# Two-layer decoder trunk on one core: a rearranged opening with seven warm-up passes, and a seventh seven-product pair in the last down projection

## The chip, the cores and the metric

The kernel runs on one core of a Trainium2 chip. The metric is the device time of one execution, in microseconds (us). The times of the kernel before are three executions; one further execution was profiled, and every row shown below comes from it.

A core has five engines that run side by side, each its own list of instructions in order: TensorE (PE in the rows; its weight loads stand as PEld), VectorE (DVE), ScalarE (ACT), GpSimd (POOL) and SyncE (SP), which here only issues DMAs. Engines wait for each other through semaphores.

## The reference

The input is 256 tokens of 1024 features in float32. Each of two layers does, with weights of its own:

```
proj  = x @ w_in                      # q,k,v of 8 heads | q,k,v of 8 heads | two gates
A     = stick_breaking_attention(...) ;  B = softmax attention with partial rotary (...)
mix   = (sigmoid(g_sb) * (A @ w_branch_sb) + sigmoid(g_mb) * (B @ w_branch_moba)) @ w_out
x     = layer_norm(alpha * x + mix)
ffn   = (silu(x @ w_gate) * (x @ w_up)) @ w_down      # inner width 2816 = 22 chunks of 128
x     = layer_norm(alpha * x + ffn)
```

## The kernel before, in words

**Numbers.** Every product is made from two parts of each operand: `hi`, the operand rounded to fp32r, and `lo`, the rest. `mm3` makes one product as three passes through TensorE: hi by hi, hi by lo, lo by hi. Weights reach the chip as granules of 128 x 1024 values (512 KB), 122 to a layer. SyncE loads a granule into one of 6 `raw` buffers, ScalarE casts it to `whi` (a ring of 10 granules, L60 in the rows) and VectorE subtracts to give `wlo` (L65). Five granules of a layer take another way: GpSimd loads them straight into `whi` by DMA, ScalarE writes `wlo = -whi`, and a second DMA adds the raw weights to it (`BY_DMA`).

**Order.** The kernel is written with a manual schedule. A small planner, `Weave`, keeps an estimated clock for each engine, and from it decides where in each engine's list the side work (splits of weights, attention, norms) stands. The chip only sees the finished lists.

**The opening.** Ten matmuls on zeros (`N_WARM`, tile `busy`) occupy TensorE while the first loads are under way. ScalarE issues four loads of x (tiles `xT_raw`, called x00, x10, x01, x11: the token block, then the part of the features), and then loads its activation table and runs a one-element activation on it (`warm`). SyncE issues the first weights in halves (w00, w01, w10, ...) and the two larger remaining parts of x (x02, x12). `START` fixes in which order ScalarE and VectorE split those pieces. The first two outputs are v of the two attention kinds (`l0pv` from granules 0 to 3, then `l0pu` from granules 4 to 7), each for two token blocks. Granule 0 is not split (`NWHOLE = 1`): `whole` multiplies raw float32 values in one matmul, which stands as two rows in the profile. After them come q and k (`l0pq`).

**The down projection of layer 2.** It has 22 chunks. A chunk taken by itself is four products (two token blocks by two halves of the columns), so 12 passes. Two chunks taken as a pair (`seven_products`) need seven products in place of eight, so 21 passes, at the price of sums of weights and of activations on VectorE (`sums_line`, and the granule kinds "t" and "u", whose weights are first added up in the raw buffers). The table `DOWN[1]` gives the order: six pairs, and the rest single. The last `HOLD` chunks come after everything else, first for token block 0, then for block 1, so that the norm of block 0 runs beside the products of block 1. `combine_line` adds the four shared sums of the pairs (`one`, `six`, `five`, `seven`) into the residual rows `x0` and `x1` while those held chunks are multiplied. `last_first` and `last_second` then do the norm of the two token blocks and store them.

In rows, `l1pd`, `l1pe` and `l1pt` are the sums in PSUM of the last down projection, `l1hs` the sums of activations, `l1sf` the activations, `l1pv` and `l1pr` scratch of `combine_line`, `l1b_...` the last norm, `ln` its gain and shift.

Of the kernel before, what the change touches and what calls it, by code (L numbers as in the profile page):

```python
# [15 lines left out]
P = 128  # L16
# [14 lines left out]
GCOLS = 1024  # L31
NG_LAYER = 122
DOWN = ((0, (4, 5), (6, 7), 1, (8, 9), 2, (10, 11), 3, (12, 13), 14, 15, 16, 17, 18, 19, 20, 21),
        (0, (4, 5), (6, 7), 1, (8, 9), 2, (10, 11), 3, (12, 13), 16, (14, 15), 17, 18, 19, 20, 21))
STEPS = [[e for d in down for e in
          ([("n", d)] if isinstance(d, int) else [("b", d[1]), ("a", d[0]), ("t", d[0]), ("u", d[0])])]
         for down in DOWN]
BASE = [sum(NG_LAYER - NFC + len(x) for x in STEPS[:l]) for l in range(DEPTH + 1)]
EARLY = [*range(4), *range(16, 20), 8, 14, 9, 15, *range(4, 8), 20, 24, 21, 25, *range(10, 14), 22, 23,
         *range(26, 40)]  # L40
NACT = 12
# [67 lines left out]
class WeightStream:  # L109
# [2 lines left out]

    def __init__(self, nc, pool, w, total, weave, rings):
        self.nc, self.pool, self.w, self.total, self.weave = nc, pool, w, total, weave
        self.loaded, self.split = 0, NWHOLE
        self.done = -1
        self.free = {-1: 0.0}
        self.current = 0
        self.rings = rings
        self._lay()  # L120
        self.dma_t = 1.7
        self.raws, self.left = [], {0: 9.0}
        self.raw, self.parts, self.there, self.ready, self.dma = {}, {}, {}, {}, {}
# [50 lines left out]
    def by_dma(self, g):  # L174

        l, r = where(g)
        return r < NG_LAYER - NFC and r in BY_DMA[l] or self.aside(g)

    def aside(self, g):

# [3 lines left out]

    def put_aside(self, l, places):

        for g, parts in zip(filter(self.aside, range(BASE[l], BASE[l + 1])), places):
            self.parts[g] = parts
            self.dma[g] = self.weave.add(self.dma_line(g), self.weave.t)

    def dma_line(self, g):

        nc, weave = self.nc, self.weave
        hi, lo = self.parts[g]
        nc.gpsimd.dma_start(hi, self.w[place(g)], max_dma_last_dim=4096)
        yield weave.t + DMA_HI
        if self.aside(g):
            e = weave.pool(weave.t, nc.gpsimd.tensor_scalar, lo, hi.bitcast(F32), -1.0, None, op0=OP.mult) + 2.7
        else:
            e = weave.act(weave.t, GCOLS, nc.scalar.mul, lo, hi.bitcast(F32), -1.0)  # L200
        yield e
        nc.gpsimd.dma_start(lo, self.w[place(g)], accum_op=OP.add, max_dma_last_dim=4096)
        self.ready[g] = weave.t + DMA_LO

# [56 lines left out]
    def piece(self, g, i, e):  # L261

        if i == 0:
            self.parts[g] = tuple(ring[:, self.place[g]:self.place[g] + GCOLS] for ring in self.rings)
        (hi, lo), t, sl = self.parts[g], self.raw[g], self._pieces(g)[i]
        n = sl.stop - sl.start
        e = self.weave.act(e, n, self.nc.scalar.copy, hi[:, sl], t[:, sl])
        self.ready[g] = self.weave.dve(e, n, self.nc.vector.tensor_sub, lo[:, sl], t[:, sl], hi[:, sl].bitcast(F32))
        if sl.stop == GCOLS:
            self.raw.pop(g)  # L270
            self.left[g] = self.ready[g]
            self.split += 1
            self.load(g + 1 + NRAW)

# [6 lines left out]
    def take(self, g):  # L281
# [3 lines left out]
        while g in self.dma and g not in self.ready:  # L285
# [6 lines left out]
RING = 10 * GCOLS + LINES  # L292
NRAW = 6
NWHOLE = 1
START = (("x00", 4.4), ("x10", 5.4), ("x01", 6.4), ("w10", 6.4), ("w11", 7.4), ("x11", 7.4), ("w20", 8.2), ("x02", 9.0),
         ("w21", 9.7), ("x12", 10.3), ("w30", 11.0), ("w31", 11.7))
BY_DMA = ((18, 24, 28, 33, 38), (18, 24, 28, 33, 38))
ASIDE = ((), ())
X_AFTER = {(2, 0): (0, 2), (2, 1): (1, 2)}
NSPLIT = 10  # L300
HOLD = (8, 5)
FINE = 4
N_WARM = 10
LEAD = 2
LOAD = 1.46
DMA_HI = 6.0
# [12 lines left out]
def place(g):  # L319

    l, r = where(g)
    if r >= NG_LAYER - NFC:
        r = NG_LAYER - NFC + STEPS[l][r - (NG_LAYER - NFC)][1]
    return l * NG_LAYER + (EARLY[r] if r < len(EARLY) else r)


# [35 lines left out]
def hybrid_trunk_kernel(ctx: ExitStack, tc: tile.TileContext, w, xT_in, x_in, ln_in,  # L362
# [85 lines left out]
    def banksB(name):  # L448
        return psB.tile([P, 2, 512], F32, tag="B", name=name)
# [47 lines left out]

    kcs = [slice(0, 2), slice(2, 4), slice(4, 8)]
    ws.side = weave.add(ws.line(), last=True)
    for t, k in ((0, 0), (1, 0), (0, 1), (1, 1)):  # L500
        load_xT(t, kcs[k], nc.scalar)
    nc.scalar.activation(warm, zero, AF.Sigmoid)

    def between(g, i):
        if (g, i) in X_AFTER:
# [4 lines left out]
    for (kind, a, b), e in START:  # L510
        if kind == "x":
            split_xT(int(a), kcs[int(b)], e)
        else:
            ws.piece(int(a), int(b), e)
    weave.t = 4.5

    def late_loads():
        nc.sync.dma_start(ident, ident_in)
# [48 lines left out]

    def tok_major(o, g, t, first, last, k0):

        if g < NWHOLE:  # L570
            return whole(o, g, t, first)
        hi, lo = ws.take(g)
        hi = hi.rearrange("p (k c) -> p k c", k=2)
        lo = lo.rearrange("p (k c) -> p k c", k=2)
        for k in range(2):
            ts = slice(t * P, (t + 1) * P)
            mm3(o, xT_hi[:, k0 + k, ts], xT_lo[:, k0 + k, ts], hi[:, k, :], lo[:, k, :],
                first and k == 0, last and k == 1)

    def both_tokens(name, g0, put):  # L580

        acc = [banksB(f"{name}{t}")[:, 0, :] if g0 == 4 else bankM(f"{name}{t}", [P, WIDTH]) for t in range(2)]
        order = ((0, 0), (1, 0), (0, 1), (1, 1), (0, 2), (1, 2), (0, 3)) if g0 <= 4 else \
            ((0, 0), (0, 1), (0, 2), (1, 0), (1, 1), (0, 3), (1, 2))
        for t, k in order + ((1, 3),):
            tok_major(acc[t], g0 + k, t, k == 0, k == 3, 2 * k)
            if t == 1:
                ws.used(g0 + k)
            if k == 3:
                put(t, acc[t])  # L590

    def feat_major(o, g):

# [332 lines left out]
    def load_gb(l, i):  # L926
        tiles = []
        for j in range(2):
            tiles.append(unit(f"ln{l}{i}{j}", [P, D]))

        def late():
            for j, a in enumerate(tiles):
                nc.sync.dma_start(a, ln_in[4 * l + 2 * i + j].partition_broadcast(P))
                ws.dma_t = max(ws.dma_t, weave.t) + LOAD

        return tiles, late
# [3 lines left out]
    for l in range(DEPTH):  # L940
# [10 lines left out]
            split_v(v_mb[t], ps)  # L951

        if l == 0:
            both_tokens(f"{L}pv", G, put_v)
            both_tokens(f"{L}pu", G + 4, put_u)
        else:
            for t in range(2):
                weave.finish(norms[:t + 1])
                pe_after(xT_ready[t])
                for j, put in enumerate((put_v, put_u)):  # L960
                    ps = bankM(f"{L}pvu{j}{t}", [P, WIDTH])
                    for i in range(4):
                        g = G + 4 * j + i
                        tok_major(ps, g, t, i == 0, i == 3, 2 * i)
                        if t == 1:
                            ws.used(g)
                    put(t, ps)
# [164 lines left out]

        pairs = [d for d in DOWN[l] if not isinstance(d, int)]
        pair_of = {c: i for i, p in enumerate(pairs) for c in p}
        raw_h, sums, h_there = {}, {}, {}

        def sums_line(i, e):

# [4 lines left out]
                                (3, b0, tmp[:, 1], OP.subtract)):  # L1143
                e = dve(e, P, nc.vector.tensor_tensor, tmp[:, j], x, y, op=op)
            if i < 2:
                both = wide_work(f"{L}hw{i}", F32R).rearrange("p a h c -> p (a h c)")[:, :GCOLS]
            elif i < 4:
                both = work.tile([P, 2, 2, S], F32R, tag=("sbq", "sbk")[i - 2],
                                 name=f"{L}hw{i}").rearrange("p a h c -> p (a h c)")
            if i < 4:  # L1150
                places = [[both[:, n * 512:(n + 1) * 512].rearrange("p (j c) -> p j c", c=P) for n in range(2)]]
            elif i == 4:
                places = [[x[:, 2:, :].rearrange("p k (j c) -> p (k j) c", c=P) for x in h_t[-1]]]
            elif i == 5:
                places = [[x[:, 0::2, P:] for x in h_t[k]] for k in (1, 2)]
            else:
                places = [[x[:, 6:, :].rearrange("p k (j c) -> p (k j) c", c=P) for x in (xT_hi, xT_lo)]]
            n = 4 // len(places)
            sums[i] = [[hi_lo[m][:, j] for hi_lo in places for j in range(n)] for m in range(2)]
            yield e  # L1160
# [75 lines left out]
        def seven_products(i, g, late_half):  # L1236
# [22 lines left out]
            into(c21, hb[:, t1], lb[:, t1], m_hi[:, one_], m_lo[:, one_])  # L1259
            ws.used(g + 3)  # L1260

        def combine_line(e):

            v, r = (small_work(f"{L}{n}", [P, 512]) for n in ("pv", "pr"))
# [1 line left out]
            e = act(e, 512, nc.scalar.copy, v, six)  # L1266
            yield e
            e = dve(e, 512, nc.vector.tensor_sub, v, one, v)
            m_free[bank_of(one)] = m_free[bank_of(six)] = residual(e, x0, halves[0], one)
            e = dve(e, 512, nc.vector.tensor_add, r, seven, v)  # L1270
            e = dve(e, 512, nc.vector.tensor_add, v, five, v)
# [7 lines left out]
        for n, d in enumerate(DOWN[l][:-HOLD[l]]):  # L1279
            if n == 5:  # L1280
                late()
            if isinstance(d, int):
                chunk(banks[0], g, d, 0)
                chunk(banks[1][:1], g, d, 1)

                def half(g=g, d=d):
                    chunk(banks[1][1:], g, d, 1)
                    ws.used(g)

                if n == 0:  # L1290
                    late_half.append(half)
                else:
                    half()
                g += 1
                continue
# [110 lines left out]
```

## Time and profile before

| | |
|---|---|
| three executions | 716.02, 716.48, 716.57 us (median 716.48) |
| the profiled execution: time, span | 716.68 us, 714.9 us |
| TensorE matmul busy, of the span | 706.7 us, 99% |
| VectorE, ScalarE, GpSimd busy | 599.5 us, 436.6 us, 35.0 us |
| moved by DMA | 141.58 MB, 198 GB/s on average |

The span reaches from the first to the last instruction; the time of an execution is about 1.8 us more. In the timeline a row has its start, its length, the engine, the source line, the operation with tiles and shapes, a count where equal rows follow each other, and in brackets how long the engine had been idle before it and what ended that. TensorE's rows overlap, since a matmul's end is modelled: its pace is read from the distance between starts.

### The profile page before, as it was taken

How to read it: one execution, taken by the hardware profiler on the slowest of the kernel's cores; microseconds unless marked ns; L12 is line 12 of the kernel's file. 1: busy time of each engine (PE TensorE's matmuls, PEld its weight loads, DVE VectorE, ACT ScalarE, POOL GpSimd, SP SyncE). 2: the span in 40 equal slices, each digit the busy share in tenths (PEclk: the TensorE clock that was granted, in tenths of full speed). 3: DMA queues.
4: the chain of work that ended last, by engine and by line, in shares of the span. 5: the costliest groups of instructions: out<-in, count | busy, mean ns of one | idle time of the engine just before them, and what ended most of it. 6: DMA issues, size and time to landing. Idle time of an engine off the chain costs nothing. (4 is left out here: it accounts for less than half of the span.)

```text
span 714.9 us, 13082 instructions
## 1 busy us (share of the span) xinstructions
PE 706.7 (99%) x5135; PEld 657.7 (92%) x5135; DVE 599.5 (84%) x920; ACT 436.6 (61%) x677; POOL 35.0 (5%) x61
## 2 busy tenths in 40 slices
PE   9999999999999999999999999999999999999995
PEld 7999999998899999988889999999888999999885
DVE  5989989797888777799887899987879878778987
ACT  5868977664565554456456787876456555544551
POOL 0200100000000000000000010000010000000002
PEclk9999999999999999999999999999999999999998
DMA  8977755565585664449559566745646856524451
GB/s 319 396 230 254 198 153 173 167 217 186 171 301 197 194 194 145 122 142 329 198 183 315 155 186 170 213 142 177 237 147 216 273 189 198 191 96 137 147 206 59
DMA packets 40526, 141.58 MB, mean 198 GB/s; under 512 B 4625, under 2 KB 5393, under 8 KB 40465
## 3 DMA queue, kind: packets, MB, share of 16 engines
q1 hardware_dynamic: 37008, 129.74, 53.1%
q0 software_dynamic: 2880, 10.49, 6.9%
q8 instruction: 40, 0.66, 0.4%
q10 hardware_dynamic: 576, 0.52, 0.2%
q14 instruction: 22, 0.17, 0.1%
HBM read 139.69 MB, written 1.05 MB: 197 GB/s over the span
## 5 line engine op out<-in xcount | busy, mean ns | idle before, releaser
L65 DVE TENSOR_TENSOR wlo<-raw,whi 128x1024 fp32r<-128x1024 f32 (+1 forms) x274 | 302.2, 1125 | 27.2 <-ACT whi L60 23.8
L60 ACT CAST whi<-raw 128x1024 fp32r<-128x1024 f32 (+1 forms) x274 | 260.2, 973 | 75.1 <-DVE raw L65 29.5
L529 PE MATMUL l0pf<-xT_hi,whi 128*128 128x256 f32 x288 | 79.6, 276 | 0.0
L529 PE MATMUL l1pf<-xT_hi,whi 128*128 128x256 f32 x288 | 79.6, 276 | 0.0
L529 PE MATMUL l0pf<-xT_lo,whi 128*128 128x256 f32 x288 | 79.5, 276 | 0.0
L529 PE MATMUL l0pf<-xT_hi,wlo 128*128 128x256 f32 x288 | 79.5, 276 | 0.0
L529 PE MATMUL l1pf<-xT_hi,wlo 128*128 128x256 f32 x288 | 79.5, 276 | 0.0
L529 PE MATMUL l1pf<-xT_lo,whi 128*128 128x256 f32 x288 | 79.5, 276 | 0.0
L529 PEld LDWEIGHTS l0pf<-xT_lo,whi 128*128 128x128 f32 x288 | 54.1, 188 | 0.0
L529 PEld LDWEIGHTS l1pf<-xT_lo,whi 128*128 128x128 f32 x288 | 54.1, 188 | 0.0
L529 PEld LDWEIGHTS l1pf<-xT_hi,whi 128*128 128x128 f32 x288 | 54.1, 188 | 0.0
L529 PEld LDWEIGHTS l0pf<-xT_hi,whi 128*128 128x128 f32 x288 | 54.1, 188 | 0.0
L529 PEld LDWEIGHTS l0pf<-xT_hi,wlo 128*128 128x128 f32 x288 | 54.1, 188 | 0.0
L529 PEld LDWEIGHTS l1pf<-xT_hi,wlo 128*128 128x128 f32 x288 | 54.1, 188 | 0.0
L529 PE MATMUL l0pg<-xT_hi,whi 128*128 128x256 f32 x128 | 35.8, 280 | 0.0
L529 PE MATMUL l1pg<-xT_hi,whi 128*128 128x256 f32 x128 | 35.8, 280 | 0.0
L529 PE MATMUL l0pg<-xT_hi,wlo 128*128 128x256 f32 x128 | 35.5, 277 | 0.0
L529 PE MATMUL l1pg<-xT_hi,wlo 128*128 128x256 f32 x128 | 35.5, 277 | 0.0
L529 PE MATMUL l1pg<-xT_lo,whi 128*128 128x256 f32 x128 | 35.5, 277 | 0.0
L529 PE MATMUL l0pg<-xT_lo,whi 128*128 128x256 f32 x128 | 35.5, 277 | 0.0
L65 DVE TENSOR_TENSOR l1sf<-l1sf,l1pf 128x256 f32<-128x256 f32 x36 | 15.1, 421 | 15.5 <-ACT l1sf L60 14.9
L60 ACT ACTIVATE l0sf<-l0pf 128x256 f32<-128x256 f32 x18 | 6.9, 385 | 31.2 <-PE l0pf L529 31.2
(485 smaller groups left out, 1941.0 us busy)
## 6 DMA issues: line engine op xcount, KB each, us to landing
raw<-in_w_dram SPq DMA_DIRECT2D x230, 512.0 KB, 4.2
whi<-in_w_dram POOLq DMA_DIRECT2D x10, 512.0 KB, 5.1
wlo<-in_w_dram POOLq DMA_DIRECT2D x10, 512.0 KB, 6.3
ln<-in_ln_dram SPq DMA_DIRECT2D x8, 512.0 KB, 5.9
raw<-in_w_dram SPq DMA_DIRECT2D x8, 256.0 KB, 4.6
x<-in_x_dram SPq DMA_DIRECT2D x2, 512.0 KB, 4.7
xT_raw<-in_xT_dram ACTq DMA_DIRECT2D x4, 128.0 KB, 4.8
xT_raw<-in_xT_dram SPq DMA_DIRECT2D x2, 256.0 KB, 5.1
```

The costliest lines, as they stand in the source:

```text
L60: f(*args, **kw)
L65: f(*args, **kw)
L529: nc.tensor.matmul(o, a, b, start=start, stop=stop)
```

## The change

1. Seven warm-up matmuls in place of ten. ScalarE loads its activation table and runs `warm` right after its first load of x, ahead of the other three.
2. Granule 0 is taken whole for token block 0 only; for block 1 it is split like the others. The two v outputs are made alternately, so the granules of the first layer now come in the order `FIRST` (0 of one, 0 of the other, 1, 1, ...), and their sums stand in two wide PSUM tiles (`banksB`). The larger parts of x are loaded two halves later, and `START` is rearranged.
3. Layer 2's down projection: a seventh pair (16, 17); the chunks 2 and 3 come by DMA into the space of `xT_hi` and `xT_lo` (`ASIDE`); four held chunks in place of five. Three of the final sums into x are done by GpSimd, after ScalarE has multiplied those rows by alpha (`alpha_line`).
4. In both layers the gain and shift of the second norm are loaded through GpSimd's queue in place of SyncE's.

```diff
-        (0, (4, 5), (6, 7), 1, (8, 9), 2, (10, 11), 3, (12, 13), 16, (14, 15), 17, 18, 19, 20, 21))
+        (0, (4, 5), (6, 7), 1, (8, 9), 2, (10, 11), (12, 13), 3, (14, 15), (16, 17), 18, 19, 20, 21))
+FIRST = [0, 16, 1, 17, 2, 18, 3, 19]
...
-            self.dma[g] = self.weave.add(self.dma_line(g), self.weave.t)
+            self.dma[g] = self.weave.add(self.dma_line(g), self.weave.t + 3.0 * i)
...
-        if self.aside(g):
-            e = weave.pool(weave.t, nc.gpsimd.tensor_scalar, lo, hi.bitcast(F32), -1.0, None, op0=OP.mult) + 2.7
-        else:
-            e = weave.act(weave.t, GCOLS, nc.scalar.mul, lo, hi.bitcast(F32), -1.0)
+        yield weave.act(weave.t, GCOLS, nc.scalar.mul, lo, hi.bitcast(F32), -1.0)
...
-START = (("x00", 4.4), ("x10", 5.4), ("x01", 6.4), ("w10", 6.4), ("w11", 7.4), ("x11", 7.4), ("w20", 8.2), ("x02", 9.0),
-         ("w21", 9.7), ("x12", 10.3), ("w30", 11.0), ("w31", 11.7))
+START = (("x00", 4.2), ("w00", 4.7), ("x10", 5.5), ("w01", 5.6), ("w10", 6.2), ("w11", 7.0), ("w20", 7.7), ("x01", 7.8),
+         ("w21", 8.3), ("x11", 8.5), ("w30", 9.4), ("w31", 10.4), ("x02", 10.6), ("x12", 11.2))
-ASIDE = ((), ())
-X_AFTER = {(2, 0): (0, 2), (2, 1): (1, 2)}
+ASIDE = ((), (2, 3))
+X_AFTER = {(3, 0): (0, 2), (3, 1): (1, 2)}
-HOLD = (8, 5)
+HOLD = (8, 4)
-N_WARM = 10
+N_WARM = 7
...
-    for t, k in ((0, 0), (1, 0), (0, 1), (1, 1)):
+    load_xT(0, kcs[0], nc.scalar)
+    nc.scalar.activation(warm, zero, AF.Sigmoid)
+    for t, k in ((1, 0), (0, 1), (1, 1)):
         load_xT(t, kcs[k], nc.scalar)
-    nc.scalar.activation(warm, zero, AF.Sigmoid)
...
-        if g < NWHOLE:
+        if g < NWHOLE and t == 0:
             return whole(o, g, t, first)
...
+        both = [banksB(f"{names[0]}{t}") for t in range(2)]
+        acc = [[two[:, n, :] for two in both] for n in range(2)]
+        for i in range(4):
+            for n in range(2):
+                for t in range(2):
+                    tok_major(acc[n][t], g0 + 2 * i + n, t, i == 0, i == 3, 2 * i)
+                    if i == 3:
+                        puts[n](t, acc[n][t])
+                ws.used(g0 + 2 * i + n)
...
-                nc.sync.dma_start(a, ln_in[4 * l + 2 * i + j].partition_broadcast(P))
+                (nc.gpsimd if i else nc.sync).dma_start(a, ln_in[4 * l + 2 * i + j].partition_broadcast(P))
...
+        def pool_add(e, x, y, op):
+            pool(e, nc.gpsimd.tensor_tensor, x, x, y, op=op)
+            weave.pool_t += 1.0
+
+        def alpha_line():
+            for x, c in ((xs[0], halves[1]), (xs[1], halves[0]), (xs[1], halves[1])):
+                act(weave.t, 512, nc.scalar.mul, x[:, c], x[:, c], ALPHA)
+                yield weave.t + 4.0
...
+            if l == DEPTH - 1:
+                w = small_work(f"{L}pw", [P, 512])
+                e2 = dve(e, 512, nc.vector.tensor_add, w, five, v)
+                pool_add(e2, x0[:, halves[1]], w, OP.subtract)
+                m_free[bank_of(one)] = m_free[bank_of(six)] = residual(e, x0, halves[0], one)
+                e = dve(e, 512, nc.vector.tensor_add, r, seven, v)
+                pool_add(e, x1[:, halves[0]], r, OP.add)
+                e = dve(e, 512, nc.vector.tensor_sub, v, five, r)
+                pool_add(e, x1[:, halves[1]], v, OP.subtract)
+                return
```

What stands in the engines' lists at three places follows. TensorE's list begins with the warm-up matmuls and goes on with the first output. Before:

```order
L487 MATMUL busy<-few 128x128 x10
L564 MATMUL l0pv_173<-raw_119,xT_raw_92 128x512 x2
L564 MATMUL l0pv_174<-raw_119,xT_raw_93 128x512 x2
L529 MATMUL l0pv_173<-whi,xT_hi 128x512
L529 MATMUL l0pv_173<-wlo,xT_hi 128x512
L529 MATMUL l0pv_173<-whi,xT_lo 128x512
```

After (`l0pv_174` is now the tile of token block 0, `l0pv_175` that of block 1):

```order
L489 MATMUL busy<-few 128x128 x7
L567 MATMUL l0pv_174<-raw_116,xT_raw_92 128x512 x2
L532 MATMUL l0pv_175<-whi,xT_hi 128x512
L532 MATMUL l0pv_175<-wlo,xT_hi 128x512
L532 MATMUL l0pv_175<-whi,xT_lo 128x512
```

Three warm-up matmuls and two raw matmuls are gone, and the split parts of granule 0 and of x10 are needed right after the first two raw matmuls.

ScalarE's list at the pair (8, 9) of layer 2's down projection, with the numbers of the granules (242 and 243 are the pair's two raw buffers, each cast twice). Before:

```order
L60 CAST whi_89<-raw242_7171 128x1024
L60 CAST whi_89<-raw243_7294 128x512
L60 CAST whi_89<-raw243_7294 128x1024
L60 CAST whi_89<-raw242_7171 128x1024
L60 CAST whi_89<-raw246_7296 128x1024
```

After:

```order
L61 CAST whi_89<-raw242_7174 128x1024
L61 CAST whi_89<-raw243_7304 128x512
L61 ACTIVATE xT_lo_86<-xT_hi_85 128x1024
L61 CAST whi_89<-raw243_7304 128x1024
L61 ACTIVATE xT_lo_86<-xT_hi_85 128x1024
L61 CAST whi_89<-raw242_7174 128x1024
```

The two activations for chunks 2 and 3 stand between the casts of this pair, and the cast of a single chunk (246) is gone.

VectorE's list after its last split of weights, with `x_87` and `x_88` the rows of the two token blocks. Before:

```order
L65 TENSOR_TENSOR l1pv<-l1pd_7404,l1pv 128x512
L65 SCALAR_TENSOR_TENSOR x_87<-x_87,l1pd_7404 128x512
L65 TENSOR_TENSOR l1pr<-l1pt_7408,l1pv 128x512
L65 TENSOR_TENSOR l1pv<-l1pt_7407,l1pv 128x512
L65 SCALAR_TENSOR_TENSOR x_87<-x_87,l1pv 128x512
L65 SCALAR_TENSOR_TENSOR x_88<-x_88,l1pr 128x512
L65 TENSOR_TENSOR l1pr<-l1pt_7407,l1pr 128x512
L65 SCALAR_TENSOR_TENSOR x_88<-x_88,l1pr 128x512
L65 SCALAR_TENSOR_TENSOR x_87,l1b_st_7735<-x_87,l1pd_7403 128x512 x2
```

After:

```order
L66 TENSOR_TENSOR l1pv<-l1pd_7414,l1pv 128x512
L66 TENSOR_TENSOR l1pw<-l1pt_7417,l1pv 128x512
L66 SCALAR_TENSOR_TENSOR x_87<-x_87,l1pd_7414 128x512
L66 TENSOR_TENSOR l1pr<-l1pt_7418,l1pv 128x512
L66 TENSOR_TENSOR l1pv<-l1pt_7417,l1pr 128x512
L66 SCALAR_TENSOR_TENSOR x_87,l1b_st_7758<-x_87,l1pd_7413 128x512 x2
```

Eight operations ahead of the norm have become five; the three sums into x that are missing stand on GpSimd now.

More of the change, by code (lines that the diff above doesn't have):

```diff
@@ L114, in __init__ @@
         self.nc, self.pool, self.w, self.total, self.weave = nc, pool, w, total, weave
-        self.loaded, self.split = 0, NWHOLE
+        self.loaded, self.split = 0, 0
         self.done = -1
@@ L176, in by_dma @@
         l, r = where(g)
-        return r < NG_LAYER - NFC and r in BY_DMA[l] or self.aside(g)
+        if r >= NG_LAYER - NFC:
+            return self.aside(g)
+        return r in BY_DMA[l]
     def aside(self, g):
@@ L185, in put_aside @@
     def put_aside(self, l, places):
-        for g, parts in zip(filter(self.aside, range(BASE[l], BASE[l + 1])), places):
+        for i, (g, parts) in enumerate(zip(filter(self.aside, range(BASE[l], BASE[l + 1])), places)):
             self.parts[g] = parts
-            self.dma[g] = self.weave.add(self.dma_line(g), self.weave.t)
+            self.dma[g] = self.weave.add(self.dma_line(g), self.weave.t + 3.0 * i)
     def dma_line(self, g):
@@ L196, in dma_line @@
         yield weave.t + DMA_HI
-        if self.aside(g):
-            e = weave.pool(weave.t, nc.gpsimd.tensor_scalar, lo, hi.bitcast(F32), -1.0, None, op0=OP.mult) + 2.7
-        else:
-            e = weave.act(weave.t, GCOLS, nc.scalar.mul, lo, hi.bitcast(F32), -1.0)
-        yield e
+        yield weave.act(weave.t, GCOLS, nc.scalar.mul, lo, hi.bitcast(F32), -1.0)
         nc.gpsimd.dma_start(lo, self.w[place(g)], accum_op=OP.add, max_dma_last_dim=4096)
@@ L269, in piece @@
         if sl.stop == GCOLS:
-            self.raw.pop(g)
-            self.left[g] = self.ready[g]
+            if g >= NWHOLE:
+                self.raw.pop(g)
+                self.left[g] = self.ready[g]
             self.split += 1
@@ L323, in place @@
         r = NG_LAYER - NFC + STEPS[l][r - (NG_LAYER - NFC)][1]
+    if l == 0 and r < len(FIRST):
+        return FIRST[r]
     return l * NG_LAYER + (EARLY[r] if r < len(EARLY) else r)
@@ L514, in hybrid_trunk_kernel @@
             ws.piece(int(a), int(b), e)
-    weave.t = 4.5
+    weave.t = 5.1
     def late_loads():
@@ L578, in tok_major, with both_tokens @@
                 first and k == 0, last and k == 1)
[L580 to L590, printed above, removed]
+    def both_tokens(names, g0, puts):
+        both = [banksB(f"{names[0]}{t}") for t in range(2)]
[7 more added lines that the diff above has]
+                ws.used(g0 + 2 * i + n)
     def feat_major(o, g):
@@ L953, in hybrid_trunk_kernel @@
         if l == 0:
-            both_tokens(f"{L}pv", G, put_v)
-            both_tokens(f"{L}pu", G + 4, put_u)
+            both_tokens((f"{L}pv", f"{L}pu"), G, (put_v, put_u))
         else:
@@ L1134, in hybrid_trunk_kernel @@
         pair_of = {c: i for i, p in enumerate(pairs) for c in p}
-        raw_h, sums, h_there = {}, {}, {}
+        raw_h, sums, h_there, wides = {}, {}, {}, []
         def sums_line(i, e):
@@ L1145, in sums_line @@
             if i < 2:
-                both = wide_work(f"{L}hw{i}", F32R).rearrange("p a h c -> p (a h c)")[:, :GCOLS]
+                both = wide_work(f"{L}hw{i}", F32R).rearrange("p a h c -> p (a h c)")
+                wides.append(both[:, GCOLS:])
             elif i < 4:
@@ L1156, in sums_line @@
             else:
-                places = [[x[:, 6:, :].rearrange("p k (j c) -> p (k j) c", c=P) for x in (xT_hi, xT_lo)]]
+                places = [[x.rearrange("p (j c) -> p j c", c=P) for x in wides]]
             n = 4 // len(places)
@@ L1268, in combine_line @@
             e = dve(e, 512, nc.vector.tensor_sub, v, one, v)
+            if l == DEPTH - 1:
[5 more added lines that the diff above has]
+                pool_add(e, x1[:, halves[0]], r, OP.add)
+                e = dve(e, 512, nc.vector.tensor_add, v, five, r)
+                pool_add(e, x1[:, halves[1]], v, OP.subtract)
+                return
             m_free[bank_of(one)] = m_free[bank_of(six)] = residual(e, x0, halves[0], one)
@@ L1281, in hybrid_trunk_kernel @@
                 late()
+                if l == DEPTH - 1:
+                    weave.start(alpha_line())
             if isinstance(d, int):
```

## The prediction

> **What bounds the kernel now.** I read the page first, for the busy shares, then what TensorE waited for, then the timeline of the two places that the change touches: the first 28 us and the last 60 us.
>
> ```profile
> span 714.9 us, 13082 instructions
> PE 706.7 (99%) x5135; PEld 657.7 (92%) x5135; DVE 599.5 (84%) x920; ACT 436.6 (61%) x677; POOL 35.0 (5%) x61
> ...
> PE busy L487 <- DVE few L484: 0.9, 1, 0.9
> ...
> 686.22:693.70 7.48, 7.48 (x34) 1.00 0.85 343
> ```
>
> TensorE is busy for 99%, and in the list of waits it has one entry, 0.9 us before its first instruction. So the time is the number of passes times their pace, plus what happens ahead of the first useful pass and behind the last one. The window row, inside the last pair, gives the pace: 33 passes start in it (the 34th reaches in from before) in 7.48 us, 0.227 us for a pass over 512 columns. A change pays only by passes that go, by an earlier start, or by a shorter tail; work on other engines costs nothing until it makes TensorE wait.
>
> The opening:
>
> ```profile
> 0.91 3.36 PE L487 MATMUL busy<-few 128*128 128x128 f32 x14 [0.91 <-DVE few L484]
> ...
> 0.91 3.97 PE L487 MATMUL busy<-few 128*128 128x128 f32 x17 [0.91 <-DVE few L484]
> ...
> 0.91 4.30 PE L487 MATMUL busy<-few 128*128 128x128 f32 x20 [0.91 <-DVE few L484]
> ...
> 4.26 0.40 ACT L60 CAST xT_hi<-xT_raw 128x256 fp32r<-128x256 f32 x1
> 5.05 0.59 PE L564 MATMUL l0pv<-raw,xT_raw 128*128 128x512 f32 x1
> 5.48 0.19 PEld L564 LDWEIGHTS l0pv<-raw,xT_raw 128*128 128x128 f32 x1 [0.24 <-DMA raw<-in_w_dram]
> 5.65 0.41 ACT L60 CAST xT_hi<-xT_raw 128x256 fp32r<-128x256 f32 x1 [0.99 <-DMA xT_raw<-in_xT_dram]
> 5.91 0.19 PEld L564 LDWEIGHTS l0pv<-raw,xT_raw 128*128 128x128 f32 x1 [0.24 <-issue]
> ...
> 12.61 0.19 PEld L529 LDWEIGHTS l0pv<-whi,xT_hi 128*128 128x128 f32 x1 [0.28 <-ACT xT_hi L60]
> 13.33 0.19 PEld L529 LDWEIGHTS l0pv<-whi,xT_lo 128*128 128x128 f32 x1 [0.43 <-DVE xT_lo L65]
> ...
> 27.97 0.28 PE L529 MATMUL l0pq<-xT_hi,whi 128*128 128x256 f32 x1
> ```
>
> The first three rows are three views, which end at 4.05, at 4.69 and open: 14 of the 20 warm-up rows have started by 4.05, 17 by 4.69, and the other three start between 4.69 and the first useful row at 5.05. So the pace is 0.21 us up to about 4.70 and 0.12 after it: TensorE runs at half speed for its first 3.8 us. x00 is there at 4.26, w01 by 5.48, x10 at 5.65. The raw rows follow at 0.43 us. v and u take 27.97 - 5.05 = 22.92 us: 8 x 0.43 = 3.44, 84 passes x 0.227 = 19.04, and 0.44 left over, which the rows at 12.61 and 13.33 explain (x12 is late).
>
> **The change part by part: the opening.** Three warm-up matmuls are six rows; without them TensorE is free at 4.06, and its first useful row waits for x00, at 4.26 in place of 5.05: -0.79. The rows from 4.26 to 4.70 run at half speed: +0.22. Two raw matmuls go (4 rows, 1.72) and six passes come (1.36): -0.36. The waits for x12 go (-0.44): its first use moves from the third granule to the fifth, past 15 us. The splits of v come some 6 us later, in banks that nobody waits for. That is -1.37 if nothing else waits, and v and u end at 26.60.
>
> What is late next is the splitting, since the alternating order needs w10 and w11 at once, and granule 0 now adds two casts and two subtractions. By the rows below a half granule costs 0.62 on ScalarE and 0.68 on VectorE behind it.
>
> ```profile
> 7.12 1.13 ACT L60 CAST whi<-raw 128x512 fp32r<-128x512 f32 x2
> 9.31 0.68 DVE L65 TENSOR_TENSOR wlo<-raw,whi 128x512 fp32r<-128x512 f32 x1
> 14.43 1.05 ACT L60 CAST whi<-raw 128x1024 fp32r<-128x1024 f32 x1 [0.63 <-DMA raw<-in_w_dram]
> 15.51 2.52 DVE L65 TENSOR_TENSOR wlo<-raw,whi 128x1024 fp32r<-128x1024 f32 x2 [0.98 <-ACT whi L60]
> 2.61 1.28 ACT L502 ACT_TABLE_LOAD   x1 [2.61 <-issue]
> ```
>
> The first raw matmul ends at 4.70 + 0.86 - 0.22 = 5.34 and the second needs w01: +0.14, to 6.34. Block 1 of granule 0: x10 is cast by 6.05, w01 by 6.67, its low part is there at 7.35, wanted at 7.25: +0.10. Granule 1: w11 is there by 7.64 (the second cast of the 7.12 row), its low part at 7.64 + 0.62 + 0.04 + 0.68 = 8.98, wanted near 8.74: +0.24. The fifth granule lands at 14.43, its low part is there at 15.51 + 1.26 = 16.77, wanted near 16.5: 0 to 0.3, I take 0.17. Together +0.65. The opening gives -1.37 + 0.65 = -0.72.
>
> The table load ahead of x10, x01 and x11 is the part that no row shows. If ScalarE goes on issuing behind a running table load, x10 leaves at 1.17 as now and nothing changes; if it waits for load and activation (1.28 + 0.20), x10 comes up to 1.5 us later, and so do its cast and the casts behind it: block 1 of granule 0 starts at 7.57 in place of 6.34, +1.23. Nor is a gain excluded: with x10, x01 and x11 out of the way, w01 to w11 land sooner and the waits shrink. I take no change, between -0.48 and +1.23.
>
> **Layer 2's down projection.** One product less is 3 passes: -0.68. Everything else must stay hidden, and VectorE is the engine to watch:
>
> ```profile
> L65 DVE TENSOR_TENSOR l1hs<-l1sf,l1hs x12: 283/288/293, 567.8 to 622.7; 128x128 f32<-128x128 f32 x12
> 635.87 0.42 DVE L65 TENSOR_TENSOR l1sf<-l1sf,l1pf 128x256 f32<-128x256 f32 x1 [1.81 <-ACT l1sf L60]
> 651.40 0.28 PE L529 MATMUL l1pf<-xT_hi,wlo 128*128 128x256 f32 x1
> 655.82 1.57 ACT L60 CAST whi<-raw 128x1024 fp32r<-128x1024 f32 x2 [1.92 <-PE l1pe L529]
> 656.91 1.83 DVE L65 TENSOR_TENSOR wlo<-raw,whi 128x1024 fp32r<-128x1024 f32 x2 [0.84 <-ACT whi L60]
> 660.28 1.06 ACT L60 CAST whi<-raw 128x1024 fp32r<-128x1024 f32 x1 [2.88 <-DVE raw L65]
> 661.56 5.38 DVE L65 TENSOR_TENSOR wlo<-raw,whi 128x1024 fp32r<-128x1024 f32 x5
> 669.76 5.38 DVE L65 TENSOR_TENSOR wlo<-raw,whi 128x1024 fp32r<-128x1024 f32 x5
> 671.26 0.39 PE L529 MATMUL l1pd<-whi,l1h_hi 128*128 128x512 f32 x1
> 686.16 2.50 DVE L65 TENSOR_TENSOR wlo<-raw,whi 128x1024 fp32r<-128x1024 f32 x2
> 692.34 0.39 PE L529 MATMUL l1pd<-whi,l1h_hi 128*128 128x512 f32 x1
> ...
> 696.80 0.68 DVE L65 TENSOR_TENSOR l1pv<-l1pd,l1pv 128x512 f32<-128x512 f32 x1
> 702.10 0.68 DVE L65 SCALAR_TENSOR_TENSOR x<-x,l1pd 128x512 f32<-128x512 f32 x1
> 706.73 2.50 POOL L70 TENSOR_TENSOR l1b_y<-l1b_y,ln 128x512 f32<-128x512 f32 x2 [0.83 <-ACT l1b_y L60]
> 707.65 0.42 DVE L65 TENSOR_TENSOR x<-x,l1b_rest 128x256 f32<-128x256 f32 x1
> DMA to landing us min/median/max: 3.7/5.1/8.3
> ```
>
> From 656.91, where the ring lets it go on (ScalarE's cast at 655.82 waits for TensorE), VectorE runs without a break; a pair with a single chunk takes 669.76 - 661.56 = 8.20 us, while TensorE needs 33 x 0.227 = 7.48. Its lead has shrunk to 692.34 - 688.66 = 3.7 us at the last pair's last product. A split is about 1.17, so a pair alone is 7.03 against 21 passes, 4.76. In before's clock (the opening's gain moves both engines): pair (8, 9) is split by 664.0; the activation for chunk 3 on ScalarE stands between its last two casts, whose gap was only 0.4, so +0.45. Four more pairs: 664.4 + 4 x 7.03 = 692.6, and +0.2 where an alpha multiplication (about 0.6, the length of a 512-wide cast) stands in front of a cast: 692.8. TensorE's last pair ends at 693.70 - 0.68 + 12 x 0.227 = 695.74, since 12 passes fewer are held back behind it, and wants that last part 6 passes earlier, at 694.4. The lead falls to 1.6 us and stays over zero: cost 0.
>
> The chunks 2 and 3: their space is free when `l1pf` ends, 651.40; the two first DMAs land after 5.1 us (the last row, of the same kind of DMA in the attention parts), near 657, when ScalarE comes to them at 657.4. The adding DMA follows; TensorE wants chunk 2 at 671. The sums of the seventh pair (four of 0.29, one 0.68) fall where VectorE sat idle before 635.9 for 1.81 us. The norm's gain and shift leave SyncE's queue, which costs nothing as GpSimd's queue is empty there.
>
> The end: block 0's held chunks are 24 passes in place of 30 and end at 695.74 + 5.44 = 701.18; they are `combine_line`'s cover. VectorE: 692.8 + 4 x 1.17 = 697.5, then five operations in 3.4: 700.9, where it came to the norm at 702.10 before, 1.2 behind TensorE (693.70 + 30 x 0.227 + 0.39). GpSimd's three sums, at 1.25 each (the 706.73 row) from 699.0, end at 702.8; block 1's rows are wanted 12 passes after 701.18, at 704. So the end is again TensorE's last pass: the sum at 707.65 moves by the full 0.68, and the tail behind it is as before. Bounds for this stage: -0.75 (a tail with less crowding on GpSimd) to +0.3 (below).
>
> **The sum.** 716.68 (the profiled execution) - 0.72 - 0.68 = 715.28. That execution is 0.20 above the median, so 715.1 for the median of the changed kernel, 1.4 below. About 0.2%, 1.43 us or 715.05, is what a measurement can tell from no change; the forecast lies at that line.
>
> **The rivals.**
>
> *The opening loses its waits.* If x10, x01 and x11 leave later without being missed, w01, w10 and w11 come sooner and most of the 0.65 goes: 715.1 - 0.5 = 714.6. For it: the loads share the DMA engines, and x01 and x11 are wanted only after 10 us now. Against it: the fifth granule's landing stays.
>
> *x10 comes late.* ScalarE's queue holds x10 until its table is loaded: +1.23 less the 0.3 that is already counted as waiting, 716.0. No row shows a DMA behind a table load on this queue.
>
> *VectorE falls behind.* The first DMA may land after 8.3 us, the longest above, at 660.1: both casts behind the activations slip, 1.5 us in all, against 0.5 of slack at the end: 715.1 + 1.0 = 716.1. Against it: that landing was seen beside a crowded DMA queue.
>
> *TensorE stays at half speed, the slower case.* The rows show full speed only after 3.8 us of unbroken passes. Now there is a gap from 4.06 to 4.26 and shorter ones at 5.34, 7.25 and 8.74. If a gap starts the count again, half speed until t costs (t - 4.70) / 2, less the 0.5 of waits that it hides. If only the first gap does, t is 8.05: +1.2, 716.3. If the one at 8.74 does too, t is about 12.5: +3.4, 718.5. It decides from t = 8.6 on. Against it: the gaps are under a tenth of the 3.8 us.
>
> [...]
>
> **How the numbers follow.** Forecast as summed 0.45 (715.1, own range 714.7 to 715.6, half of it below 715.05); opening without waits 0.20; x10 late 0.12; VectorE behind 0.10; half speed once 0.08, twice 0.05. Faster: 0.22 + 0.20 = 0.42. Slower by over 0.2%: the twice-half-speed case, and a little of the once-case with other waits, 0.07. Same: the rest, 0.51. The range leaves out the slower case above and the tail of the best below: 714.2 to 716.7.
>
> **What would show it.** Right: first useful row near 4.3, `l0pq` near 27.2, no wait for x12, the pair (16, 17) in 21 passes, the last sum on `l1b_rest` 1.4 earlier, VectorE reaching the last norm before TensorE's block 0 ends. Wrong: the cast of x10 after 6.5; raw rows at 0.86 apart; a wait of TensorE in the pairs after 686; GpSimd's sums ending after 704.

## The result, and the profile after

The changed kernel is slower: 721.12 us (median of six, 719.65 to 723.07) against 716.88 for the kernel before (six, 716.02 to 717.75). The ratio is 1.0059, interval 1.0048 to 1.0070. The prediction, 715.1 in a range up to 716.7, was wrong: 1.4 us less were forecast, and 4.2 more were measured. The profiled execution is the longest of the six, 723.07 us with a span of 721.3; its sums are made against the 714.9 of before.

TensorE's waits, which were only the warm-up's start before, now have a large entry (engine, tile and line that waited, what it waited for; total, times, longest):

```profile
PE l0pv L532 <- DVE l0vsb L66: 5.2, 1, 5.2
PE busy L489 <- DVE few L486: 0.9, 1, 0.9
PE l0pv L532 <- DVE wlo L66: 0.2, 1, 0.2
```

The place in the timeline, TensorE's rows of the changed kernel (start, length, idle time before in brackets):

```profile
25.24 0.39 PE L532 MATMUL l0pv<-whi,xT_lo 128*128 128x512 f32 x1
30.80 0.80 PE L532 MATMUL l0pv<-whi,xT_hi 128*128 128x512 f32 x1 [5.17 <-DVE l0vsb L66]
31.39 0.63 PE L532 MATMUL l0pv<-wlo,xT_hi 128*128 128x512 f32 x1
31.81 0.63 PE L532 MATMUL l0pv<-whi,xT_lo 128*128 128x512 f32 x1
...
35.08 0.28 PE L532 MATMUL l0pq<-xT_hi,whi 128*128 128x256 f32 x1
```

The row at 25.24 is v's last pass. The next 12 passes are u's last granule. Both outputs are called `l0pv` here, since they share the two wide tiles: v in the first half, u in the second. Before u's pass can start, VectorE must have subtracted for `l0vsb`, the low part of v: 30.80 - 25.24 - 0.23 = 5.33 us lost. Then the starts stand 0.43 apart instead of 0.227 until about 33.5, and the 12 passes take 35.08 - 30.80 = 4.28 in place of 2.72: another 1.56. Why the subtraction is so late stands in ScalarE's and VectorE's rows of the same stretch:

```profile
24.56 1.05 ACT L61 CAST whi<-raw 128x1024 fp32r<-128x1024 f32 x1 [0.16 <-DMA raw<-in_w_dram]
27.16 2.37 ACT L61 CAST whi<-raw 128x512 fp32r<-128x512 f32 x4 [1.55 <-DMA raw<-in_w_dram]
29.44 1.06 ACT L61 CAST l0vsb<-l0pv 128x512 fp32r<-128x512 f32 x2
30.05 0.69 DVE L66 TENSOR_TENSOR l0vsb<-l0pv,l0vsb 128x512 fp32r<-128x512 f32 x1 [0.95 <-ACT l0vsb L61]
```

v is complete in PSUM at about 25.6. Its cast stands in ScalarE's list behind the casts of granules 12 and 13 (the row x4), and these wait for a load that comes at 27.1. TensorE goes on when the subtraction of 30.05 ends.

Behind the opening the profile after is the predicted one; what else was off in the opening itself follows further down. Four stretches of the opening, with busy times of PE, PEld, DVE, ACT and POOL, granted clock, DMA share and GB/s, show a granted clock near a half in one of them only:

```profile
7.00:25.00 18.00, 17.83 (x78) 14.23 (x77) 14.26 (x18) 12.76 (x18) 2.58 (x8) 1.00 0.99 371
25.00:31.00 6.00, 0.83 (x4) 0.39 (x3) 4.11 (x6) 4.35 (x9) 0.00 (x0) 0.95 1.01 391
31.00:34.00 3.00, 3.00 (x8) 2.38 (x9) 2.74 (x5) 0.78 (x3) 0.00 (x0) 0.52 0.78 273
34.00:36.00 2.00, 2.00 (x14) 1.78 (x13) 1.62 (x3) 2.00 (x5) 0.00 (x0) 1.00 0.82 254
```

And the end of layer 2, rows of all engines:

```profile
658.64 0.28 PE L532 MATMUL l1pf<-xT_hi,wlo 128*128 128x256 f32 x1
697.49 7.05 DVE L66 TENSOR_TENSOR wlo<-raw,whi 128x1024 fp32r<-128x1024 f32 x6
708.59 1.28 POOL L71 TENSOR_TENSOR x<-x,l1pv 128x512 f32<-128x512 f32 x1
708.62 0.69 DVE L66 SCALAR_TENSOR_TENSOR x<-x,l1pd 128x512 f32<-128x512 f32 x1 [0.77 <-PE l1pd L532]
714.21 0.42 DVE L66 TENSOR_TENSOR x<-x,l1b_rest 128x256 f32<-128x256 f32 x1 [0.16 <-PE l1b_rest L532]
```

From the last `l1pf` to the last sum on `l1b_rest` it takes 714.21 - 658.64 = 55.57, before 707.65 - 651.40 = 56.25: 0.68 less. VectorE now waits 0.77 for TensorE ahead of the last norm, where it came 1.2 late before.

The difference of the spans by place: start to `l0pq` +7.11 (27.97 before, 35.08 after), `l0pq` to the first down pass of layer 2 +0.14, down passes -0.68, the rest behind them -0.17. Sum +6.40.

### The profile page after: what moved, and what is told of

Same layout as the page of the kernel before. It is cut to its first block, busy times and chain, and to the rows that moved or that the text cites. A ratio compares the mean times of both kernels' runs of the same rounds, so it can differ in the third digit from the quotient of the medians.

```text
span 721.3 us, 13103 instructions
## 1 busy us (share of the span) xinstructions
PE 707.8 (98%) x5128; PEld 658.3 (91%) x5128; DVE 602.8 (84%) x928; ACT 440.6 (61%) x685; POOL 42.5 (6%) x72
```

## The experiments

Each was timed beside the kernel before on the same chip. Theory A: a write to one half of a wide tile waits until the splits have read the other half. Theory B: the stall belongs to the alternate order and its late splits, whatever tiles are used.

**own_banks: u in tiles of its own**

```diff
-        both = [banksB(f"{names[0]}{t}") for t in range(2)]
-        acc = [[two[:, n, :] for two in both] for n in range(2)]
+        acc = [[banksB(f"{names[0]}{t}")[:, 0, :] for t in range(2)],
+               [bankC(f"{names[1]}{t}", [P, WIDTH]) for t in range(2)]]
```

> Changed kernel, v's sums in the first half of the wide tiles, u's sums in two one-bank tiles of the other pool, order of the passes and all else as it is. Theory A (u's last passes write the tile from which the splits of v still read, so TensorE stands still until VectorE has subtracted): no wait of TensorE for l0vsb and no half-speed passes behind it; l0pq starts at 35.08 - 5.33 - 1.54 = 28.2 instead of 35.08. Against the kernel before that is +0.24 in the opening and -0.68 in layer 2: about 716.4 us, where the changed kernel has 721.1. Rival B (the stall belongs to the alternate order itself, because the splits of v stand behind weight splits that wait for their loads): the stall stays, over 720 us.

Measured: 717.11 us, ratio to the kernel before 1.0000 (0.9991 to 1.0008). The stall and the half speed behind it are gone:

```profile
26.63 0.39 PE L532 MATMUL l0pu<-whi,xT_lo 128*128 128x512 f32 x1
26.85 0.28 PE L532 MATMUL l0pq<-xT_hi,whi 128*128 128x256 f32 x1
...
32.55 0.63 PE L546 MATMUL turn_tp<-ident,tab 128*128 128x128 f32 x4 [2.00 <-issue]
```

The passes and the splits stand in the lists in the same order as in the changed kernel, so B falls. But a new wait stands at 32.55, 2.0 us that were not expected: `turn_tp` takes its tile from the pool in which u now stands. The trace names nothing that ended this wait (`issue`), but in TensorE's list an instruction just ahead of `turn_tp` waits for VectorE's subtraction for u's first rows, which runs from 31.77 to 32.45.

**own_banks_m: v in the tiles that l0pq wants next**

```diff
-        both = [banksB(f"{names[0]}{t}") for t in range(2)]
-        acc = [[two[:, n, :] for two in both] for n in range(2)]
+        acc = [[bankM(f"{names[0]}{t}", [P, WIDTH]) for t in range(2)],
+               [banksB(f"{names[1]}{t}")[:, 0, :] for t in range(2)]]
```

> As own_banks, but v's sums in the two tiles of the pool from which l0pq takes its tile next, u's in the first half of the wide tiles. Theory A: the splits of v stay as late as they are (the first subtraction ends near 30.7); u's last passes run through, and the wait moves on to l0pq, which wants that tile at 28.2 and gets it at 30.8: +2.6 against own_banks, 719.0 us, and up to 1.5 more if the idle time brings half speed again: 719.0 to 720.5. Rival B: as the changed kernel, 721.

Measured: 716.93 us, 0.9999 (0.9990 to 1.0008). The wait moved to `l0pq` as A has it. It is 1.98 us (29.03 - 26.82 - 0.23) where 2.6 were expected: the load came earlier in this execution and v's first cast with it (27.68 against 29.44), while `l0pq` was wanted at 27.05 in place of 28.2.

```profile
26.82 0.39 PE L532 MATMUL l0pu<-whi,xT_lo 128*128 128x512 f32 x1
29.03 0.38 PE L532 MATMUL l0pq<-xT_hi,whi 128*128 128x256 f32 x1 [1.82 <-DVE l0vsb L66]
```

No half speed follows an idle time of 1.8 us: from 29.25 on the passes of 256 columns start 0.11 to 0.12 apart. In own_banks and own_banks_m the tiles decide who waits for the late splits; in neither do the splits stand earlier in the lists. Each has one wait of about 2 us, at another place, and so the two take the same time, where 2.6 us between them were expected.

**dma_est: earlier splits, wide tiles kept**

```diff
-        self.dma_t = 1.7
+        self.dma_t = 6.0
```

> Changed kernel with its wide tiles, but the planner's estimate of the first load's time 4.3 us later, so that the splits of v stand two weight granules earlier in ScalarE's and VectorE's lists. Theory A: u's last passes still wait for the splits of v, but only 0.9 us for the first and 0.5 for the second, too short for half speed if that follows from the long wait: l0pq near 29.6, about 717.8 us. If sharing the tile costs whatever stands ahead of the splits, the 5.3 us stay: 721.

Measured: 717.89 us, 1.0008 (0.9999 to 1.0016).

```profile
23.93 0.39 PE L532 MATMUL l0pv<-whi,xT_lo 128*128 128x512 f32 x1
24.77 0.50 PE L532 MATMUL l0pv<-whi,xT_hi 128*128 128x512 f32 x1 [0.46 <-DVE l0vsb L66]
```

The shared tile still costs a wait, 24.77 - 23.93 - 0.23 = 0.61 us, and 0.24 for the second rows. The 5 us need both: a shared tile, and splits that stand behind a load. (The edit moves the planner's estimate for every load, so other splits move along with those of v.)

**before_wide: the old order in wide tiles**

```diff
+    wide2 = []
...
-        acc = [banksB(f"{name}{t}")[:, 0, :] if g0 == 4 else bankM(f"{name}{t}", [P, WIDTH]) for t in range(2)]
+        if g0 == 0:
+            wide2.extend(banksB(f"{name}{t}") for t in range(2))
+        acc = [wide2[t][:, g0 // 4, :] for t in range(2)]
```

> Kernel before, in its own order (all of v, then all of u), with nothing changed but the place of the sums: v's in the first half, u's in the second half of the same two wide tiles. Theory A (a write to one half waits until the splits have read the other half): u's first passes, wanted near 20.4, wait for VectorE's subtraction for v's first rows, which ended at 21.08; one wait of TensorE for l0vsb of 0.5 to 0.8 us, none for the second rows, l0pq near 28.6 instead of 27.97: 717.9 us against 717.2. Rival: the halves lie in different banks and have nothing to do with each other: no wait, 717.2.

Measured: 722.76 us, 1.0079 (1.0067 to 1.0091). The same wait in the old order, so the tile is the cause and the alternate order is not needed for it. The size was far off: I had taken the start of u from the late cast of v; TensorE wanted u at 17.6, not 20.4. Two rows of the timeline:

```profile
17.38 0.39 PE L529 MATMUL l0pv<-whi,xT_lo 128*128 128x512 f32 x1
21.00 0.80 PE L529 MATMUL l0pv<-whi,xT_hi 128*128 128x512 f32 x1 [3.23 <-DVE l0vsb L65]
```

and two stretches, with the granted clock as third number from the end:

```profile
17.50:21.00 3.50, 0.27 (x3) 0.01 (x1) 3.40 (x4) 3.31 (x6) 0.00 (x0) 0.90 1.05 407
21.00:27.00 6.00, 6.00 (x14) 4.80 (x15) 5.97 (x7) 4.95 (x7) 4.14 (x8) 0.50 1.00 405
```

21.00 - 17.38 - 0.23 = 3.39 us of wait bring another 6 us at a granted clock of 0.50, so about 3 us more are lost.

**opening_only and layer2_only: the two parts by themselves**

opening_only is the kernel before with parts 1 and 2 of the change, layer2_only with parts 3 and 4.

> Kernel before with the opening's part of the change alone (idle passes, order of the loads, alternate order, wide tiles), layer 2 as before. If the whole loss is the opening's and layer 2's part gives its 0.68: TensorE's wait for l0vsb of 3 to 5 us, half speed behind it, 717.2 + 4.2 + 0.7 = 722.1 us. Rival: the parts hang together (the adding DMA or GpSimd's queue makes the stall longer): 720 to 721.

> Kernel before with the part for layer 2 alone (the seventh pair, chunks 2 and 3 by DMA, the three sums on GpSimd, the norm's gain and shift on GpSimd's queue). My account of the prediction: one product less, 3 passes, -0.68, all else hidden: 716.2 us against 716.9. Rival: the part costs as much as it saves (VectorE or GpSimd late at the end), 716.9, and the whole loss of 4.2 us is then the opening's minus nothing.

Measured: opening_only 722.82 us, 1.0077 (1.0064 to 1.0090); layer2_only 716.29, 0.9983 (0.9974 to 0.9992). Against the kernel before beside them that is +5.7 and -1.0, together +4.7, where the whole change has +4.2. The down passes of layer2_only take 0.68 less, as in the changed kernel, so the loss is the opening's alone. opening_only waits as well, in the list of waits:

```profile
PE l0pv L534 <- DVE l0vsb L66: 3.9, 1, 3.9
```

Its stretches behind that wait, the granted clock third from the end:

```profile
29.00:30.50 1.50, 1.22 (x5) 1.04 (x6) 1.50 (x4) 1.03 (x2) 0.00 (x0) 1.00 1.03 423
30.50:34.00 3.50, 3.50 (x9) 2.34 (x9) 3.50 (x6) 1.62 (x3) 0.00 (x0) 0.51 0.80 259
```

**filler: TensorE kept busy in the wait**

```diff
+N_FILL = 16
...
+                for _ in range(N_FILL if (i, n) == (3, 1) else 0):
+                    nc.tensor.matmul(busy, zero.to_broadcast([P, P]), zero.to_broadcast([P, P]), start=True, stop=True)
```

> Changed kernel with 16 more idle matmuls (32 short rows, 3.6 us at full clock) in TensorE's list between v's last pass and u's last passes, where it stands still. The wait itself stays, since the splits of v don't move. If the half speed behind the wait follows from the standstill, it is gone: no rows at 0.43 us after the wait, 1.5 us won against the changed kernel, about 719.9 us where the kernel before has 717.2. If it comes from something else (the load on the other engines, the casts), rows at 0.43 stay and so does the time, 721.4.

Measured: 720.26 us, 1.0046 (1.0033 to 1.0059); the interval overlaps the changed kernel's 1.0048 to 1.0070, so the time alone doesn't tell. The trace does: the wait is there, and no half speed follows (granted clock 1.00 from 27 to 33 us, where the changed kernel has 0.52 from 31 to 34). (The profiled execution is the longest of its five, 721.49 us, and has one more wait, 1.3 us in layer 2's attention, which the changed kernel's profile doesn't show.)

```profile
24.09 3.73 PE L591 MATMUL busy<-few 128*128 128x128 f32 x32
28.92 0.50 PE L533 MATMUL l0pv<-whi,xT_hi 128*128 128x512 f32 x1 [1.09 <-DVE l0vsb L66]
29.26 0.40 PE L533 MATMUL l0pv<-wlo,xT_hi 128*128 128x512 f32 x1
```

**est5_own_m, late_a, est5_own_m_w10: the repaired opening**

All three have the tiles of own_banks_m. est5_own_m has `self.dma_t = 5.0`, est5_own_m_w10 also `N_WARM = 10`, and late_a shifts the estimate for four granules only:

```diff
-            self.there[g] = self.dma_t + 1.0
+            self.there[g] = self.dma_t + (1.0 + 3.3 if 12 <= g < 16 else 1.0)
```

> Changed kernel with v's sums in the two one-bank tiles that l0pq and l0pk take next, u's in the first half of the wide tiles, which nobody takes next, and the planner's estimate of the first load's time 3.3 us later, so that v's first split stands ahead of the weight granule whose load comes late (27.1). Theory: with early splits and tiles of their own no wait of TensorE is left in the opening: l0pq near 26.9 as in own_banks, which had its 2.2 us wait only later; 686.2 us from there to the end: 714.9 us against 717.2. Rival: the wait moves on once more (l0pq for v's first subtraction, or the attention part for weights split later): 716 to 717.

> As est5_own_m, with 10 idle matmuls instead of 7, so that the idle passes run on until the first data are there, without a gap. If the gap between idle passes and first useful row does not matter for the clock (own_banks_m had full speed from 4.5 with a gap, layer2_only only from 6.6 without one), the useful work only starts later, at 5.05 instead of 4.4: +0.3 to +0.65, 715.4 us. If the gap holds the clock down, this kernel gains up to 1.0: 714.0.

> As est5_own_m, but the planner's estimate of the load's time is later by 3.3 us for granules 12 to 15 alone, so that the order of the splits changes in the opening and nowhere else. est5_own_m took 624.4 us from l0pq to the last down projection, where kernels with the old estimate took 623.5 to 624.0. If its moved splits cost that, this kernel gains 0.4 to 0.9 on it: 715.2 us against 717.2 of the kernel before. If l0pq waits for v's first subtraction (near 27.4, wanted near 27), 0.4 of it is lost again: 715.6 to 715.9.

Measured: 715.87 us, 0.9983 (0.9974 to 0.9991); with ten warm-up passes 716.29, 0.9990 (0.9981 to 0.9999); late_a 715.71, 0.9982 (0.9973 to 0.9991). The opening of est5_own_m has no wait for splits any more:

```profile
27.39 0.39 PE L532 MATMUL l0pu<-whi,xT_lo 128*128 128x512 f32 x1
27.62 0.28 PE L532 MATMUL l0pq<-xT_hi,whi 128*128 128x256 f32 x1
```

All three beat both kernels, but by less than expected. est5_own_m reached `l0pq` 0.7 later than assumed, since its first raw rows ran at half speed (2.75 us for the four, against 2.03 in own_banks_m), and took 624.4 us from there to layer 2's down passes, the kernel before 623.5. late_a took 623.55 there, which suggests that the wider shift of the splits costs some of it; these are single executions. late_a's own profiled execution waited 1.77 us at 16.4 for the fifth granule's split. The three warm-up passes are worth 0.4 between the medians, which fits the expectation, with overlapping intervals; a gain of 1.0 for the run without a gap is out. Against layer2_only the repaired opening adds nothing that these intervals can tell.

**l2_no_aside and l2_sums_dve: what layer 2's helpers are worth**

Both are edits of layer2_only:

```diff
-ASIDE = ((), (2, 3))
+ASIDE = ((), ())
```

```diff
-            pool(e, nc.gpsimd.tensor_tensor, x, x, y, op=op)
-            weave.pool_t += 1.0
+            dve(e, 512, nc.vector.tensor_tensor, x, x, y, op=op)
```

> layer2_only with chunks 2 and 3 through the usual path instead of the DMAs: two loads on SyncE's queue, two casts on ScalarE and two subtractions of 1.23 on VectorE more, behind which the last pairs come. VectorE's lead was 1.6 us at the last pair; by the account of the prediction it turns into a lag of 0.9, and TensorE waits for wlo in the last pairs: 0.7 to 1.2 us, 717.2 us where layer2_only has 716.3. Rival (the lead is larger than that account makes it, or the ring, not VectorE, sets the pace): no wait, 716.3.

> layer2_only with the three last sums on VectorE instead of GpSimd: 3 x 0.69 us more on VectorE, which came to the last norm 0.75 us before TensorE was done there, so it is now 1.3 late. By the account of the prediction that is hidden again, as 1.2 us were in the kernel before, because block 1's last passes go on for 5 us: 716.3 to 716.6 us. Rival (the norm of block 0 is on the path): +1.3, 717.6.

Measured: 721.57 us, 1.0061 (1.0049 to 1.0074), and 717.53, 1.0005 (0.9996 to 1.0014), where layer2_only has 0.9983. So layer 2's part gains nothing without either helper, and both expectations were too low. Without the DMAs the last split comes to stand behind `combine_line`'s operations, and TensorE waits for it in a held chunk:

```profile
PE l1pd L527 <- DVE wlo L65: 2.7, 1, 2.7
```

and VectorE's rows in the timeline:

```profile
701.65 0.69 DVE L65 TENSOR_TENSOR l1pv<-l1pt,l1pr 128x512 f32<-128x512 f32 x1
702.26 1.89 DVE L65 TENSOR_TENSOR wlo<-raw,whi 128x1024 fp32r<-128x1024 f32 x1
```

and TensorE's, which goes on at full speed, 0.23 to 0.24 us from start to start behind the first pass:

```profile
701.14 0.39 PE L527 MATMUL l1pd<-whi,l1h_hi 128*128 128x512 f32 x1
704.21 0.50 PE L527 MATMUL l1pd<-wlo,l1h_hi 128*128 128x512 f32 x1 [2.67 <-DVE wlo L65]
704.54 0.40 PE L527 MATMUL l1pd<-whi,l1h_lo 128*128 128x512 f32 x1
704.78 0.39 PE L527 MATMUL l1pd<-whi,l1h_hi 128*128 128x512 f32 x1
```

The wait is most of the 3.7 us by which this execution's span exceeds layer2_only's. The other four executions are 0.7 to 1.9 us longer still; what they lost is open.

With the sums on VectorE the down passes take their 55.14 us as in layer2_only, but from the last pass's start to the end it takes 8.6 instead of 7.4: VectorE runs without a break from 690 to 712 and ends last. The 1.2 us are not hidden; the rival was right.

## Why the prediction was wrong, point by point

**The step that failed.** "The splits of v come some 6 us later, in banks that nobody waits for", priced at nothing. u's last 12 passes wait for them, in the same tiles. That cost 5.33 + 1.56 = 6.89 us in the profiled execution. It is the longest of the six, and the others have no profile. The shortest, 719.65 us, shows a mean granted clock of 0.999 against 0.994, so it can have lost little to half speed; how long it waited is open. I had treated the halves as separate because they are different banks. TensorE's list in the changed kernel would have told (`Activation_49` and `DVE_49` are the counters of ScalarE and VectorE): at each earlier granule of u the first pass waits for a cast (ScalarE) and the second for a subtraction (VectorE); at the last granule it is the first pass that waits for VectorE:

```
59 L532 MATMUL l0pv_174<-whi,xT_hi 128x512 [waits Activation_49]
60 L532 MATMUL l0pv_174<-wlo,xT_hi 128x512 [waits DVE_49]
...
83 L532 MATMUL l0pv_174<-whi,xT_hi 128x512 [waits DVE_49]
84 L532 MATMUL l0pv_174<-wlo,xT_hi 128x512
```

In the list of own_banks the same pass waits for ScalarE, like the earlier ones. So the wait is one that the program carries for a shared tile; these runs don't show a limit of PSUM itself.

v and u had different banks; the wait in before_wide, 3.23 us, shows that different banks alone do not keep the next write from waiting in a kernel like this one, where both banks are one tile.

**The opening's other terms.** Without the stall `l0pq` would stand at 35.08 - 6.89 = 28.19, +0.22 to before, where -0.72 was forecast. The term that is off is the half speed, which was to end at 4.70. These are the first rows of the changed kernel:

```profile
0.91 3.35 PE L489 MATMUL busy<-few 128*128 128x128 f32 x14 [0.91 <-DVE few L486]
4.40 3.04 PE L567 MATMUL l0pv<-raw,xT_raw 128*128 128x512 f32 x4
```

and of own_banks_m, with the same instructions:

```profile
0.91 3.36 PE L489 MATMUL busy<-few 128*128 128x128 f32 x14 [0.91 <-DVE few L486]
4.47 2.03 PE L567 MATMUL l0pv<-raw,xT_raw 128*128 128x512 f32 x4 [0.21 <-DMA xT_raw<-in_xT_dram]
```

The four raw rows took 3.04 us and 2.03. With the second `l0pq` would have come 0.79 earlier than before; own_banks_m, less its wait, reaches `l0pq` at 29.03 - 1.98 = 27.05, where 27.25 was forecast. So the sum of the opening came within 0.2 us for an execution that comes to full speed early, in part by luck: its first useful row stands 0.21 later than forecast, since x00 came later, and the 0.22 of half speed behind it was not paid. By the distance between starts, the waits that I had priced at 0.14, 0.10 and 0.24 are 0.15, 0.14 and 0.10 there. Nothing waited for x12, as forecast, and the fifth granule's wait was 0.44 in the changed kernel, against 0.17.

**The rival of the late x10.** Refuted: the three loads are issued while the table is loaded (ACTq are ScalarE's DMA issues), and x10 is cast at 5.86, before at 5.65.

```profile
1.17 1.28 ACT L503 ACT_TABLE_LOAD   x1 [1.17 <-PEq L1417]
1.23 1.35 ACTq L492 DMA_DIRECT2D xT_raw<-in_xT_dram  x3
```

**The rival of the half speed** had the right place in the opening's start, but as an effect of gaps it is not borne out: own_banks_m has the gap and full speed from 4.5, and layer2_only (below) has none and half speed until 6.5. The half speed that cost 1.56 came from a long wait that no rival had; filled with short passes, it brought none (filler, granted clock 1.00 behind it). The chances that this rival was given, 0.08 and 0.05, were my estimate: no row of the kernel before shows what a gap does to the pace.

**Layer 2.** Right: 0.68, hidden work included. VectorE's last split ends at 704.54, which is 697.30 in before's clock (7.24 earlier, by the last `l1pf`), forecast 697.5; it waits for TensorE ahead of the norm; and GpSimd's last sum ends at 709.87, 702.63 in before's clock, forecast 702.8. That VectorE fell behind, a rival, did not happen.

## What to carry to other kernels

Where two accumulators share one PSUM tile in a kernel like this one, emptying one holds up the next write to the other, even in another bank (by 5.33 us in the changed kernel, 3.39 in before_wide, 0.61 in dma_est): give them tiles of their own, and ask of each tile who writes it next, not only who reads it. Work priced at nothing because it is late but unwanted needs its reader and its next writer checked in the instruction lists, where the wait stands in plain sight. In these runs the waits of TensorE of 3.2 us and more cost more than their length: about 3 us more in before_wide, 33.81 - 29.28 - 2.72 = 1.81 in opening_only, 1.56 in the changed kernel.

## What the runs showed of the hardware

**When the clock falls.** Idle times of 1.8, 2.0 and 2.7 us (own_banks_m, own_banks, l2_no_aside) left full speed: the passes soon behind them start 0.11 to 0.12 apart over 256 columns and 0.23 to 0.24 over 512. Those of 3.2, 3.9 and 5.2 us (before_wide, opening_only, the changed kernel) were followed by about 6, 3 and 3 us at a granted clock of 0.50, 0.51 and 0.52. The filler's 3.7 us of short passes in the wait kept full speed, at a granted clock of 1.00. In opening_only the work first ran on at full speed for 1.3 us, from 29.28 to 30.55; no run shows why. By the distance between starts the longest of these idle times that left full speed is 704.21 - 701.14 - 0.23 = 2.84 us and the shortest that lost it 3.39.

**When it rises.** The opening of the kernel before, the same instructions in three kernels, came to full speed at about 4.7 (before), 3.9 (l2_sums_dve) and 6.5 (layer2_only), in the rows of the warm-up passes and the raw rows. It is read from their pace, since the granted clock does not show it: it stands at 1.00 from 0.90 to 9.00 in the kernel before and from 4.70 to 9.00 in layer2_only. First those of l2_sums_dve:

```profile
0.91 3.88 PE L485 MATMUL busy<-few 128*128 128x128 f32 x20 [0.91 <-DVE few L482]
4.62 3.60 PE L562 MATMUL l0pv<-raw,xT_raw 128*128 128x512 f32 x8
```

and those of layer2_only:

```profile
0.91 4.64 PE L485 MATMUL busy<-few 128*128 128x128 f32 x20 [0.91 <-DVE few L482]
5.34 4.17 PE L562 MATMUL l0pv<-raw,xT_raw 128*128 128x512 f32 x8
```

`l0pq` stands at 27.41 in the first of these and at 28.44 in the second: 1.0 us between executions of the same opening, more than the 0.72 that this part of the change was to win. One profile can't show the end of the half speed to better than that.
